# Weight sums and their stores held in program order, ten steps apart, begun one group of weights later, in a streaming encoder step

## The chip, the core and the metric

The kernel runs on one core of one Trainium2 chip. The metric is the device time of one execution in microseconds (us), as the median of several executions. Engines are called by their names or by the profile's short ones: TensorE (PE, with PEld for its weight loads), VectorE (DVE), ScalarE (ACT), GpSimd (POOL), SyncE (SP). A letter q behind a name means the engine's sequencer, which issues DMAs.

## What is computed

One inference step of one encoder layer, in float32, for two groups of requests that share the weights: a prompt of 2048 rows and 8 samples of 16 rows, 17 tiles of 128 rows of width 1024 in all.

```python
h = rms_norm(x, norm_g[0])
z = h @ w_in                       # 1024 x 3592, split among the heads
att = band_attention(...)          # 8 heads of 64, own chunk of 64 and 8 before it
hb = mlstm(...)                    # 4 heads of 128, a matrix memory along the sequence
x = x + rms_norm(concat(att, mlstm_out) @ w_out, norm_g[1])
u = rms_norm(x, norm_g[2]) @ w_up  # 1024 x 5632
y = b_conv + causal_conv3(u)
x = x + rms_norm((gelu(y_gate) * y_up) @ w_down, norm_g[3])
```

Caches and states are outputs too. The change touches none of the arithmetic.

## The kernel before, in words

Every float32 product is made as three products of high and low parts in a rounded format (`mm3`, lines 95 to 97): of each weight that is loaded, ScalarE makes the high part and VectorE the low one.

The two products of the FFN use seven block products in place of eight (a scheme after Strassen), and so need sums and differences of quarters of `w_up` and `w_down`. These do not depend on the data, but they are inputs' sums and have to be made in the kernel: `weight_sums` makes them once, while the first part of the layer runs, and writes them to DRAM (`wsd` and `wtd`), from where the FFN loads them later. Each of the 22 blocks of `w_up` and 11 of `w_down` is one unit. A unit has four loads of a quarter (128 x 512, line 1189, on SyncE's queue, into buffers `wsum0` to `wsum3` with two copies each), four combines (`tensor_tensor` on VectorE, line 1193, each in place, the later ones using the results of the earlier) and four stores (line 1197, on SyncE's queue). A table `acts` says in which step of a generator each of these is called: four loads in four steps, the combines eleven steps behind the loads, the stores three steps behind the combines, and the next unit eleven steps behind this one.

The first part of the layer is a loop over 28 groups of weights (14 groups of columns of `w_in`, for each half of the rows; `seq`). A group's product yields after every half of an accumulation: 18 or 16 times for a group of row tiles (`va`, `vo`), 12 times for a transposed one (`qk`, `qb`). At each yield the loop calls one step of the next group's load (line 1163, with its split at 1169 and 1170), one step of the weight sums, sometimes one of a row tile's norm (`norm_tile`, load at 214, Square on ScalarE at 218, scaling on VectorE at 221, then eight transposes on TensorE), and then `pump`, which lets steps of two other streams go: attention (loads of a head's `qraw`, `kraw` and `vraw` at 336, 339 and 353, split at 344 to 358, scores and softmax at 384 to 421) and the matrix memory (lines 640 to 790). A step of the sums counts as no work there, so the order in which everything else is called does not depend on the sums.

What is called is not yet the order on the engines. A scheduler takes all instructions, and by a timing model of its own puts each on its engine's queue when it holds it to be ready, mostly in the order of calls. Each engine then works through its queue in order. `tc.keep_in_program_order(ins)` adds one edge: `ins` does not come ahead of the one instruction that was called before it on the same engine. It adds no wait, and that other instruction itself may still be moved ahead of its own predecessors. The loads of the sums already have this edge.

At the end of the loop come the output projection (`wo`) with the norms, and then the FFN in three blocks of rows (`ua`, `ub`, `uec` are the accumulators of its first product, `dnm` and `dn` of its second).

Of the kernel before, what the change touches and what calls it, by code (L numbers as in the profile page):

```python
# [44 lines left out]
def hymba_step(ctx: ExitStack, tc: tile.TileContext, I: dict, O: dict):  # L45
    nc = tc.nc
# [213 lines left out]
    def group_rows(wh, wl, half, chunks, dst, name, width=256, out=None):  # L260
        for ci, tiles in enumerate(HALVES[half]):
            for j, t in enumerate(tiles):
                ch = chunks[ci]
                acc = ps_mm(f"{name}_{t}")
                for k in range(KT):
                    w = slice(k * width, (k + 1) * width)
                    tt = slice(j * P, (j + 1) * P)
                    mm3(acc[:, :width], ch[:, 0, k, tt], ch[:, 1, k, tt], wh[:, w], wl[:, w],
                        start=(k == 0), stop=(k == KT - 1))
                    if k % 4 == 3:  # L270
                        yield 1.3, 0.0
                stage = pa.tile([P, 384], F32, tag="st", name=f"{name}_st{t}", bufs=2)
                evac_scaled(stage[:, :256], acc[:, :256], None)
                if width > 256:
                    nc.vector.tensor_copy(gates[:, gate_ix(t), :], acc[:, 256:width])
                s = 4 if t == SAMPLE else t // 4
                nc.scalar.dma_start(dst[s][:, 0 if s == 4 else t % 4, :], stage[:, :256])
                if out is not None and s >= 3:
                    nc.scalar.dma_start(out[s - 3][:, 0 if s == 4 else t % 4, :], stage[:, :256])
# [536 lines left out]
    def prep(units):  # L816
        yield units
        yield FLUSH
# [230 lines left out]
    def quad(name):  # L1049
        return ffn.p3.tile([P, 512], F32, tag="q", name=name, bufs=11)  # L1050
# [101 lines left out]
    def load_group(gi):  # L1152

        i = SRC[GROUPS[gi]]
        src, n = (I["w_in0"], 2112) if i == 0 else (I["w_in1"][i - 1], 2048)
        h = wpool.tile([P, 2112], F32R, tag="wh", name=f"wi{i}_h{gi}", bufs=2)
        l = wpool.tile([P, 2112], F32R, tag="wl", name=f"wi{i}_l{gi}", bufs=2)

        def steps():
            q = n // 2  # L1160
            for s in range(2):
                raw = pr.tile([P, 1056], F32, tag="wraw", name=f"wi{i}_raw{s}")
                nc.sync.dma_start(raw[:, :q], src[:, s * q:(s + 1) * q])
                yield 0.0, 0.0
                yield 0.0, 0.0
                for e in range(2):
                    c = slice(s * q + e * q // 2, s * q + (e + 1) * q // 2)
                    r = raw[:, e * q // 2:(e + 1) * q // 2]
                    nc.scalar.copy(h[:, c], r)
                    nc.vector.tensor_tensor(l[:, c], r, h[:, c], op=ALU.subtract)  # L1170
                    yield 0.0, 0.6

        return h, l, steps()

    def weight_sums():


        add, sub = ALU.add, ALU.subtract
        up = ((2, 3, 2, add), (3, 0, 3, sub), (0, 2, 0, sub), (1, 1, 0, sub))
        down = ((0, 1, 0, sub), (1, 2, 1, sub), (2, 2, 0, sub), (3, 3, 2, sub))  # L1180
        todo = [(I["w_up"][f], wsd[f], up, f"u{f}") for f in range(NF)]
        todo += [(I["w_down"][i], wtd[i], down, f"d{i}") for i in range(NF // 2)]
        acts = defaultdict(list)
        for n, (src, dst, plan, nm) in enumerate(todo):
            t = []

            def load(i, src=src, t=t, nm=nm):
                t.append(pr.tile([P, 512], F32, tag=f"wsum{i}", name=f"wsum{nm}_{i}", bufs=2))
                tc.keep_in_program_order(nc.sync.dma_start(t[i], src[:, i * 512:(i + 1) * 512]))

            def combine(e, plan=plan, t=t):
                o, x, y, op = plan[e]
                nc.vector.tensor_tensor(t[o], t[x], t[y], op=op)

            def store(e, dst=dst, plan=plan, t=t):
                o = plan[e][0]
                nc.sync.dma_start(dst[:, o * 512:(o + 1) * 512], t[o])

            for i in range(4):
                acts[11 * n + i].append(lambda i=i, f=load: f(i))  # L1200
                acts[11 * n + 11 + i].append(lambda i=i, f=combine: f(i))
                acts[11 * n + 14 + i].append(lambda i=i, f=store: f(i))
        for step in range(max(acts) + 1):
            for act in acts[step]:
                act()
            yield 0.0, 0.0

    def norm_steps(half):

        for ci, tiles in enumerate(HALVES[half]):  # L1210
            ch = phT.tile([P, 2, KT, 384], F32R, tag="hT", name=f"hT{half}_{ci}", bufs=3)
            chunks.append(ch)
            for j, t in enumerate(tiles):
                norm_tile(t, ch, j, ps_big)
                yield 0.9, 2.5
# [10 lines left out]
    next(norms)  # L1226
    load_bias()
    sums = weight_sums()
    for n_, (half, gi) in enumerate(seq):
        wh, wl, _ = pend  # L1230
        split = iter([])
        if n_ + 1 < len(seq):
            pend = load_group(seq[n_ + 1][1])
            split = pend[2]
        g = GROUPS[gi]
        i = int(g[2])
        nm = f"{g}_{half}"
        if g[:2] == "va":
            it = group_rows(wh, wl, half, chunks, vd[i], nm, 264 if gi == 0 else 256,
                            [O["v_prompt"][i], O["v_sample"][i].unsqueeze(1)])  # L1240
        elif g[:2] == "qk":
            it = group_T(wh, wl, half, chunks, [qTd[i], kTd[i]], [-(DA ** -0.5), None], nm,
                         [None, [O["k_prompt"][i], O["k_sample"][i]]])
        elif g[:2] == "qb":
            it = group_T(wh, wl, half, chunks, [[t_[:, c, :] for t_ in qkbd[i]] for c in range(2)],
                         [None, DH ** -0.5], nm)
        else:
            it = group_rows(wh, wl, half, chunks, vobd[i], nm)
        if half == 0 and gi == 13:
            chunks = []  # L1250
            norms = norm_steps(1)
        if n_ == len(seq) - 1:
            out = project([0, 1, 2, 3, 4, 5, 6, 7, SAMPLE, 8, 9, 10, 11, 12, 13, 14, 15])
            split = w_out_steps()
            next(split)
            next(out)
        for u, (pe, dve) in enumerate(it):
            ahead = []
            if n_ < len(seq) - 1 or u >= 6:
                ahead.append(next(split, (0.0, 0.0)))  # L1260
            if n_ == len(seq) - 1 and u == 12:
                ahead.append(next(out))
            if n_:
                ahead.append(next(sums, (0.0, 0.0)))
            if (half == 0 and gi == 13 and u >= 6 and u % 2 == 0) or (gi == 0 and u % 2 == 0):
                ahead.append(next(norms, (0.0, 0.0)))
            pump(pe + sum(a[0] for a in ahead), dve + sum(a[1] for a in ahead))
        for _ in split:
            pass
        if n_ == len(seq) - 1:  # L1270
            for _ in sums:
                pass
        if gi == 0:
            if half == 0:
                nc.sync.dma_start(bgate, I["b_gate"].broadcast_to([P, 8]))
                nc.sync.dma_start(gatt, I["g_att"])
                heads.append(build_bias)
                mems.append(lambda: prep(prep_sample()))
            mems.append(lambda half=half: prep(prep_prompt(half)))
        if g[:2] == "qk":  # L1280
            attention(i, half)
            if half == 0 and i == 3:
                heads.insert(len(heads) % 4, lambda: attention_sample(0, EARLY))
            if half == 1 and i == 0:
                heads.insert(len(heads) % 4, lambda: attention_sample(EARLY, DB))
        if g[:2] == "vo":
            mems.append(lambda i=i, half=half: mlstm(i, half))
            if half == 0:
                mems.append(lambda i=i: mlstm_sample(i))
# [145 lines left out]
    for b, tiles in enumerate(FBLOCKS):  # L1435
        last = b == len(FBLOCKS) - 1
        nt = len(tiles)
        n = HALF[b]
# [180 lines left out]
        if not last:  # L1619
# [4 lines left out]
            for q in range(42):  # L1624
# [25 lines left out]
                for j in range(3):  # L1650
# [4 lines left out]
                    elif p == D2:  # L1655
                        o = quad(f"c11_{b}_{j}")
# [7 lines left out]
                    elif p == D4:  # L1664
                        o = quad(f"c21_{b}_{j}")
# [160 lines left out]
```

## Time and profile before

| | us |
|---|---|
| median of 3 runs | 2860.12 |
| lowest, highest | 2860.08, 2869.72 |
| the profiled execution | 2870.22 |
| its span in the trace | 2868.5 |
| mean granted clock of TensorE in it | 0.982 |

The profile comes from one execution, whose own time is 2870.22 us; its span, from the first instruction to the last, is 2868.5 us. In a table of stretches each engine has its busy time in us with the number of instructions in brackets, then PEclk, the mean clock that TensorE was granted as a share of full speed, the busy share of the DMA engines, and GB/s. A row of waits reads: engine, what it wants to write and at which line, then who was waited for; the total in us, how often, and the longest. A row of the timeline reads: start, length, engine, line, operation, output and inputs, count, and in square brackets how long the engine had been idle before, and what released it.

### The profile page before, as it was taken

The page shows a single profiled execution, that of the slowest core. Times are in us where ns is not written, and L with a number is a line of the kernel's source. Part 1 is how long each engine was busy: PE and PEld are TensorE (multiplying, and loading weights), DVE is VectorE, ACT ScalarE, POOL GpSimd, SP SyncE. Part 2 cuts the span into 40 slices and gives each one's busy share as a digit, 9 for nine tenths or more (in the row PEclk, how much of TensorE's full clock was granted, in tenths as well). Part 3 has the DMA queues.
Part 4 walks back from the last instruction along what each step waited for, and adds up shares of the span by engine and source line. Part 5 has one row for each costly group of instructions (what it writes and reads, how often), then busy time and mean ns, then how long its engine had stood idle before and what let it go on. Part 6 is the DMA issues. An engine that isn't in the chain of part 4 may idle for free.

```text
span 2868.5 us, 47580 instructions
## 1 busy us (share of the span) xinstructions
PE 2726.6 (95%) x16389; PEld 2540.8 (89%) x16389; DVE 1977.6 (69%) x3640; ACT 1439.0 (50%) x2908; POOL 436.3 (15%) x876
## 2 busy tenths in 40 slices
PE   7899999989889999898999999999999999999998
PEld 7799999888889997776899998889999878999877
DVE  5355555656656567676588888858888885888765
ACT  4254544534435556553355555754545565555543
POOL 1000000111100001223411110011111121222221
PEclk9999999999999999998999999999999999999999
DMA  5755567568877576435565556774555797555586
GB/s 172 221 170 175 173 194 219 184 213 266 270 255 218 166 212 210 141 100 165 190 211 179 165 181 200 265 226 155 175 177 166 244 324 245 171 177 180 170 297 204
DMA packets 371346, 575.50 MB, mean 201 GB/s; under 512 B 60611, under 2 KB 176799, under 8 KB 370975
## 3 DMA queue, kind: packets, MB, share of 16 engines
q1 hardware_dynamic: 332510, 538.62, 59.6%
q10 hardware_dynamic: 38592, 33.83, 3.5%
q8 instruction: 129, 2.11, 0.3%
q14 instruction: 115, 0.93, 0.1%
HBM read 424.24 MB, written 151.21 MB: 201 GB/s over the span
## 4 chain that ended last, share of the span: by engine, by line
PE 49%; DVE 3%; DMA 3%; issue 2%; ACT 1%; POOL 1%; SPq 0%; DVEq 0%; ACTq 0%; POOLq 0%
PE uec L95 6%; PE uec L96 6%; PE uec L97 6%; PE ua L97 3%; PE ua L96 3%; PE ua L95 3%; PE dn L95 3%; PE dn L97 3%; PE dn L96 3%; PE dnm L97 2%; PE dnm L95 2%; PE dnm L96 2%; PE ub L96 1%; PE ub L97 1%; PE ub L95 1%
## 5 line engine op out<-in xcount | busy, mean ns | idle before, releaser
L95 PE MATMUL uec<-B,wuh 128*128 128x384 f32 (+1 forms) x720 | 234.3, 327 | 1.5 <-DVE uu L1451 1.5
L96 PE MATMUL uec<-B,wuh 128*128 128x384 f32 (+1 forms) x720 | 235.2, 327 | 0.0
L97 PE MATMUL uec<-B,wul 128*128 128x384 f32 (+1 forms) x720 | 234.2, 327 | 0.0
L1298 ACT CAST wuh<-wu 128x512 fp32r<-128x512 f32 x315 | 172.9, 617 | 81.0 <-PE uec L96 79.2
L1299 DVE TENSOR_TENSOR wul<-wu,wuh 128x512 fp32r<-128x512 f32 x315 | 202.9, 685 | 2.9 <-DMA x2d<-mx 2.9
L95 PE MATMUL dn<-wdh,gh 128*128 128x512 f32 x422 | 168.1, 398 | 12.0 <-ACT gh L1298 9.0
L96 PE MATMUL dn<-wdl,gh 128*128 128x512 f32 x422 | 168.1, 398 | 0.0
L97 PE MATMUL dn<-wdh,gl 128*128 128x512 f32 x422 | 163.9, 402 | 0.2 <-DVE gl L1299 0.2
L95 PE MATMUL vo<-wi_h,hT 128*128 128x256 f32 x544 | 157.3, 289 | 3.4 <-ACT vo_st L226 3.3
L96 PE MATMUL vo<-wi_l,hT 128*128 128x256 f32 x544 | 156.4, 287 | 0.0
L97 PE MATMUL vo<-wi_h,hT 128*128 128x256 f32 x544 | 155.2, 285 | 0.0
L1299 DVE TENSOR_TENSOR wdl<-wdr,wdh 128x512 fp32r<-128x512 f32 x198 | 128.4, 697 | 30.7 <-ACT wdh L1298 30.6
L95 PE MATMUL qk<-hT,wi_h 128*128 128x384 f32 (+1 forms) x384 | 130.8, 341 | 11.2 <-ACT qk_st L226 8.3
L408 DVE TENSOR_TENSOR ptl<-pt,pth 128x640 fp32r<-128x640 f32 (+4 forms) x128 | 93.4, 736 | 68.3 <-ACT pth L407 67.6
L396 ACT ACTIVATE tmp<-tmp,mn 128x640 f32<-128x640 f32 (+4 forms) x128 | 97.6, 763 | 84.8 <-DVE mn L395 78.4
L1298 ACT CAST wdh<-wdr 128x512 fp32r<-128x512 f32 x198 | 111.9, 618 | 54.1 <-DMA wdr<-in_w_down 22.5
L95 PEld LDWEIGHTS uec<-B,wuh 128*128 128x128 f32 x720 | 135.0, 188 | 2.7 <-DVE uu L1451 2.5
L96 PEld LDWEIGHTS uec<-B,wuh 128*128 128x128 f32 x720 | 135.2, 188 | 0.1
L97 PEld LDWEIGHTS uec<-B,wul 128*128 128x128 f32 x720 | 135.1, 188 | 0.0
L96 PE MATMUL qk<-hT,wi_h 128*128 128x384 f32 (+1 forms) x384 | 130.3, 339 | 0.0
L97 PE MATMUL qk<-hT,wi_l 128*128 128x384 f32 (+1 forms) x384 | 130.1, 339 | 0.0
L95 PE MATMUL qb<-hT,wi_h 128*128 128x384 f32 (+1 forms) x384 | 127.8, 333 | 1.9 <-ACT qb_st L228 1.1
(428 smaller groups left out, 8904.9 us busy)
## 6 DMA issues: line engine op xcount, KB each, us to landing
wu<-wsd SPq DMA_DIRECT2D x264, 256.0 KB, 3.8
wu<-in_w_up SPq DMA_DIRECT2D x198, 256.0 KB, 4.0
wdr<-in_w_down SPq DMA_DIRECT2D x110, 256.0 KB, 6.1
wi_raw<-in_w_in SPq DMA_DIRECT2D x52, 512.0 KB, 5.8
gq<-gsd SPq DMA_DIRECT2D x62, 384.0 KB, 5.2
wsumu<-in_w_up SPq DMA_DIRECT2D x88, 256.0 KB, 5.2
wsd<-wsumu SPq DMA_DIRECT2D x88, 256.0 KB, 4.4
wdr<-wtd SPq DMA_DIRECT2D x88, 256.0 KB, 6.0
```

The source lines that it names most:

```text
L95: nc.tensor.matmul(out, ah, bh, start=start, stop=False, skip_group_check=onto)
L96: nc.tensor.matmul(out, ah, bl, start=False, stop=False, skip_group_check=onto)
L97: nc.tensor.matmul(out, al, bh, start=False, stop=stop, skip_group_check=onto)
L396: nc.scalar.activation(tmp[:, :n], tmp[:, :n], AF.Exp, bias=mn, scale=-1.0, accum_out=rsum[:, i % 4, hh:hh + 1])
L408: nc.vector.tensor_tensor(s.ptl[:, sl, qc], ptv, s.pth[:, sl, qc], op=ALU.subtract)
L1298: nc.scalar.copy(h, r)
L1299: nc.vector.tensor_tensor(l, r, h, op=ALU.subtract)
```

## The change

Four things change in the sums, and nothing else in the code:

- the combine and the store get `keep_in_program_order`, as the loads have it;
- units are called 10 steps apart instead of 11 (the combines stay 11 steps behind the loads of their unit);
- the stores are called two steps behind their combines instead of three;
- the sums begin with the third group of weights instead of the second (`n_ > 1`), 30 yields after the start instead of 18. 32 intervals of 10 and the last store's 16 steps make 337 steps, from yield 30 to 367; before it was 32 × 11 + 17 + 1 = 370 steps, from 18 to 388, of 396.

```diff
             def combine(e, plan=plan, t=t):
                 o, x, y, op = plan[e]
-                nc.vector.tensor_tensor(t[o], t[x], t[y], op=op)
+                tc.keep_in_program_order(nc.vector.tensor_tensor(t[o], t[x], t[y], op=op))
 
             def store(e, dst=dst, plan=plan, t=t):
                 o = plan[e][0]
-                nc.sync.dma_start(dst[:, o * 512:(o + 1) * 512], t[o])
+                tc.keep_in_program_order(nc.sync.dma_start(dst[:, o * 512:(o + 1) * 512], t[o]))
 
             for i in range(4):
-                acts[11 * n + i].append(lambda i=i, f=load: f(i))
-                acts[11 * n + 11 + i].append(lambda i=i, f=combine: f(i))
-                acts[11 * n + 14 + i].append(lambda i=i, f=store: f(i))
+                acts[10 * n + i].append(lambda i=i, f=load: f(i))
+                acts[10 * n + 11 + i].append(lambda i=i, f=combine: f(i))
+                acts[10 * n + 13 + i].append(lambda i=i, f=store: f(i))
...
-            if n_:
+            if n_ > 1:
                 ahead.append(next(sums, (0.0, 0.0)))
```

The scheduler moves other instructions with these, since its model of the time changes. Three places show it. The first is SyncE's queue near the start, in the first group of weights, before: `xr_710` is the load of the sample's rows, `wi_raw` are halves of the next groups' weights, `wsumu_0` to `wsumu_2` the quarters of the first unit (a number at the end of a name only counts the tiles made).

```order
L1163 DMA wi_raw_822<-in_w_in 128x1024
L1189 DMA wsumu_0_824<-in_w_up 128x512
L1189 DMA wsumu_1_838<-in_w_up 128x512
L1189 DMA wsumu_2_899<-in_w_up 128x512
L214 DMA xr_710<-in_x_sample 128x1024
L1163 DMA wi_raw_963<-in_w_in 128x1024
```

And the same place of SyncE's queue after:

```order
L1163 DMA wi_raw_822<-in_w_in 128x1024
L214 DMA xr_710<-in_x_sample 128x1024
L1163 DMA wi_raw_955<-in_w_in 128x1024
L304 DMA relrow<-ext 128x767 x4
L327 DMA nb_0_1246<-relrow 128x640
L327 DMA nb_0_1317<-relrow 128x640
L1163 DMA wi_raw_1159<-in_w_in 128x1024
L1189 DMA wsumu_0_1161<-in_w_up 128x512
```

The first unit's loads, which stood ahead of the sample's rows, now stand five loads of other things behind them. On ScalarE's queue the Square of those rows (line 218) has at the same time moved ahead by one tile: it now stands in front of the copy of the accumulator `va_0_5` (line 226), where it stood in front of that of `va_0_6`.

The second place is VectorE's queue in the first of the matrix memory's heads (`num`, `ad` and `cst` belong to it), near 425 us in the profile of before; `wi_l` is a low part of weights. Before:

```order
L706 TENSOR_TENSOR num_4_4598<-num_4_4598,ma_4_1_4635 128x129
L640 SCALAR_TENSOR_TENSOR ad_4_4672<-num_4_4598 128x2
L1193 TENSOR_TENSOR wsumu_2_4802<-wsumu_3_4835,wsumu_2_4802 128x512
L641 TENSOR_TENSOR ad_4_4672<-ad_4_4672,colsp 128x2
L1170 TENSOR_TENSOR wi_l_5910<-wi_raw_5924,wi_h_5909 128x512
```

The same place of VectorE's queue after:

```order
L703 SCALAR_TENSOR_TENSOR cst_319<-cst_319,dec_1119,ma_4_1_4635 128x129
L694 TENSOR_TENSOR w_6_1_4667<-ms_6_1_4664,w_6_1_4667 128x128
L494 TENSOR_SCALAR hgms_4909<-hgms_4909 128x128
L884 RECIPROCAL srs_4291<-srs_4291 128x1
L706 TENSOR_TENSOR num_4_4597<-num_4_4597,ma_4_1_4635 128x129
L640 SCALAR_TENSOR_TENSOR ad_4_4672<-num_4_4597 128x2
L641 TENSOR_TENSOR ad_4_4672<-ad_4_4672,colsp 128x2
```

The combine between the two steps of `ad` is gone from there; combines of other units stand elsewhere in the queue.

The third place is SyncE's queue where a unit's stores (`wsd`) stand among the loads of attention heads (`qraw`, `kraw`, `vraw`), in the third pair of weights' columns. Before:

```order
L1197 DMA wsd_241<-wsumu_3_1929 128x512
L336 DMA qraw_0_2102<-qTd_0_99 64x512 x2
L339 DMA kraw_0_0_2103<-kTd_0_82 64x512 x2
L1197 DMA wsd_241<-wsumu_0_1804 128x512
L1197 DMA wsd_241<-wsumu_1_1840 128x512
```

After, in that region:

```order
L1197 DMA wsd_240<-wsumu_2_1826 128x512
L1189 DMA wsumu_3_2282<-in_w_up 128x512
L353 DMA vraw_1_1_2349<-vd_1_115 128x4x64
L1197 DMA wsd_240<-wsumu_0_1743 128x512
L336 DMA qraw_1_2465<-qTd_1_100 64x512 x2
L339 DMA kraw_1_0_2466<-kTd_0_82 64x512 x2
```

A store stands ahead of a head's loads in both; in the new order the stores of a unit are spread more among them.

## The prediction

> **What bounds the kernel now.** I read the page's busy line first, then the table of stretches, then who waits for whom on VectorE and SyncE, and last the timeline around TensorE's gaps.
>
> ```profile
> PE 2726.6 (95%) x16389; PEld 2540.8 (89%) x16389; DVE 1977.6 (69%) x3640; ACT 1439.0 (50%) x2908; POOL 436.3 (15%) x876
> core 0: us, PE busy (x) PEld busy (x) DVE busy (x) ACT busy (x) POOL busy (x), PEclk, DMA share, GB/s
> 0.00:40.00 40.00, 29.09 (x217) 27.99 (x218) 26.83 (x41) 24.09 (x39) 9.21 (x31) 1.00 0.70 221
> 40.00:130.00 90.00, 72.99 (x397) 68.88 (x397) 30.57 (x98) 18.62 (x42) 1.32 (x6) 0.89 0.62 180
> 130.00:1330.00 1200.00, 1117.51 (x7643) 1052.49 (x7643) 720.36 (x1633) 597.95 (x1455) 144.60 (x335) 0.98 0.64 197
> 1330.00:2868.50 1538.50, 1507.00 (x8137) 1391.46 (x8135) 1199.84 (x1869) 798.32 (x1374) 281.19 (x505) 0.99 0.63 204
> ```
>
> TensorE sets the time, so the change is worth what it takes out of TensorE's gaps and out of the stretches with a low granted clock. The sums live in the first 1110 us (rows below); behind 1330 us the order of instructions changes in a few dozen rows only. From 40 to 1330 us TensorE is idle for (90 − 73.0) + (1200 − 1117.5) = 99.5 us. That is the whole stock from which a gain can come, beside the clock.
>
> ```profile
> DVE wsumu L1193 <- DMA wsumu<-in_w_up: 60.0, 26, 7.7
> DVE wsumd L1193 <- DMA wsumd<-in_w_down: 13.4, 8, 3.4
> SPq L1197 <- DVE wsumu L1193: 36.4, 23, 4.8
> SPq L1189 <- DMA wsd<-wsumu: 15.2, 11, 2.8
> L1193 DVE TENSOR_TENSOR wsumu<-wsumu,wsumu x88: 669/691/694, 91.6 to 815.8; 128x512 f32<-128x512 f32 x88
> L1193 DVE TENSOR_TENSOR wsumd<-wsumd,wsumd x44: 670/691/851, 816.6 to 1104.3; 128x512 f32<-128x512 f32 x44
> ```
>
> VectorE stands still 60.0 + 13.4 = 73.4 us in front of a combine whose load has not landed: the scheduler had put the combine right behind its load. A combine itself takes 0.691 us, and the number of combines stays 132, so no work goes; only the standing can go.
>
> **The change, part by part.** *Combines tied to program order.* The combine now stands where the code calls it, eleven steps behind its load, unless the one instruction that it is tied to has itself been moved up. That hole matters: in the listing of the order with semaphores, 80 of 132 combines name a DMA's semaphore before and 48 after. So at least 1 − 48/80 = 40% of the waits go, and at most all, since some of the 48 find their load landed long ago. I take 70%. What a wait costs TensorE is read at the places where a gap follows it:
>
> ```profile
> 427.17 0.69 DVE L1193 TENSOR_TENSOR wsumu<-wsumu,wsumu 128x512 f32<-128x512 f32 x1 [1.90 <-DMA wsumu<-in_w_up]
> 430.44 0.35 PE L700 MATMUL ma<-cst,mqk 128*128 128x129 f32 x1 [1.54 <-DVE cst L703]
> 432.04 0.44 PE L67 MATMUL spt<-ident,stmp 128*128 128x128 f32 x2 [0.91 <-ACT stmp L882]
> 583.84 0.69 DVE L1193 TENSOR_TENSOR wsumu<-wsumu,wsumu 128x512 f32<-128x512 f32 x1 [1.69 <-DMA wsumu<-in_w_up]
> 586.13 0.39 PE L97 MATMUL va<-wi_h,hT 128*128 128x264 f32 x1 [2.10 <-DVE hT L201]
> 815.78 0.69 DVE L1193 TENSOR_TENSOR wsumu<-wsumu,wsumu 128x512 f32<-128x512 f32 x1 [7.75 <-DMA wsumu<-in_w_up]
> 816.59 3.01 DVE L1193 TENSOR_TENSOR wsumd<-wsumd,wsumd 128x512 f32<-128x512 f32 x4
> 820.26 0.79 PE L96 MATMUL sot<-svl,sph 128*128 128x512 f32 x1 [2.50 <-DVE svl L904]
> 828.30 0.49 PE L95 MATMUL sot<-svh,sph 16*128 16x512 f32 x1 [1.22 <-ACT svh L903]
> ```
>
> The gaps add up to 1.54 + 0.91 + 2.10 + 2.50 + 1.22 = 8.3 us; the other waits, most of the 73.4 us, are followed by no gap, because TensorE had matmuls of the dense projection to go on with. Behind three of these places the granted clock falls to about a half:
>
> ```profile
> 46.90:57.10 10.20, 6.67 (x23) 6.27 (x24) 2.75 (x4) 1.79 (x5) 0.74 (x2) 0.51 0.08 27
> 432.60:436.00 3.40, 3.40 (x19) 3.40 (x18) 2.28 (x9) 2.34 (x10) 1.63 (x6) 0.54 0.95 265
> 586.20:589.60 3.40, 3.40 (x17) 3.40 (x18) 2.10 (x8) 0.77 (x3) 0.00 (x0) 0.54 0.55 104
> 818.30:825.10 6.80, 4.84 (x17) 4.36 (x18) 3.62 (x6) 0.00 (x0) 1.20 (x3) 0.52 0.89 287
> 122.00:125.40 3.40, 3.40 (x14) 3.40 (x13) 0.00 (x0) 0.48 (x1) 0.00 (x0) 0.54 0.99 349
> ```
>
> The loss is the length times one minus the clock: 3.40 × 0.46 = 1.6 us twice and 6.80 × 0.48 = 3.3 us, together 6.5. So this part holds 8.3 + 6.5 = 14.8 us, and 70% of it is 10.3 us (bounds 5.9 and 14.8).
>
> The Trainium skill, "TensorE: Matmul & The Clock Gate", section "What's actually happening", says the clock is halved after at least one idle window of about 3.4 us. By that rule gaps of 0.9 to 2.5 us would cost no clock and this part would be worth 70% of the gaps alone. The rows at 432.60 and 586.20 speak against it: 2.45 us of gaps and a single one of 2.10 us are each followed by 3.4 us at 0.54.
>
> *Begun one group later.* Before, three loads of the first unit stand on SyncE's queue right ahead of the sample's rows:
>
> ```profile
> 34.63 1.37 SPq L1189 DMA_DIRECT2D wsumu<-in_w_up  x3
> 36.27 0.67 SPq L214 DMA_DIRECT2D xr<-in_x_sample  x1
> 39.18 0.37 ACT L226 COPY va_st<-va 128x256 f32<-128x256 f32 x1 [1.88 <-PE va L97]
> 45.90 1.06 ACT L218 ACTIVATE hT<-xr 128x1024 fp32r<-128x1024 f32 x1 [6.35 <-DMA xr<-in_x_sample]
> 49.33 0.47 PE L67 MATMUL hT_pt<-ident,xr 128*128 128x128 f32 x1 [4.39 <-DVE xr L221]
> wu<-wsd SPq DMA_DIRECT2D x264, 256.0 KB, 3.8
> wsumu<-in_w_up SPq DMA_DIRECT2D x88, 256.0 KB, 5.2
> ```
>
> Now they stand behind it. Three times 256 KB at the 221 GB/s of that stretch is 3.6 us by which the rows land sooner: the Square starts at 45.90 − 3.6 = 42.3. But the scheduler now puts that Square ahead of the copy that was made at 39.18, so the copy slips to 42.3 + 1.06 = 43.4 and ends at 43.7. TensorE, which began its last row tile when it finished the one before (half of the way from the copy's 39.2 to 49.33 − 4.39 = 44.9, about 42.0), now begins it at 43.7, 1.7 us later, and ends at 46.7. The transposes follow at once: 49.33 − 46.7 = 2.6 us gained. Of the 10.20 × 0.49 = 5.0 us lost behind that gap at half clock I take half, 2.5. Sum 5.1 us; the bounds are 0 (the copy's new wait eats it) and 4.39 + 5.0 = 9.4.
>
> *Fewer of its transfers around 120 us.* Here ScalarE waits for an attention head's loads, with sums' loads in flight beside them:
>
> ```profile
> 117.60 2.14 DVE L1193 TENSOR_TENSOR wsumu<-wsumu,wsumu 128x512 f32<-128x512 f32 x3 [4.70 <-DMA wsumu<-in_w_up]
> 120.23 0.62 ACT L348 CAST kh<-kraw 128x512 fp32r<-128x512 f32 x1 [7.66 <-DMA vraw<-vd]
> 121.59 0.45 PE L95 MATMUL qk<-hT,wi_h 128*128 128x384 f32 x1 [4.28 <-ACT qk_st L226]
> ```
>
> This gap with its 3.40 × 0.46 = 1.6 us of clock is 5.9 us. The sums' traffic is delayed there by one group but not gone, and VectorE's wait is beside the chain, not in it; I take a third, 2 us (bounds −2, for the same loads falling on the next head, and 5.9).
>
> *Ten steps instead of eleven, stores two steps behind their combine.* The same 132 loads, combines and stores in 330 instead of 363 steps: VectorE's share for them rises by a tenth for as long as they run, from 132 × 0.691 = 91 us in the 1013 us between 91.6 and 1104.3, 9.0%, to 9.9%. VectorE is busy 720 of 1200 us there, so I cost it at nothing; if that cover is gone it is 0.9% of those 1013 us, 9 us at most. The sums end some 20 steps sooner, which only frees VectorE.
>
> *Stores tied to program order.* SyncE works its queue in order, and behind a store that waits for its combine stand the loads of the next head and of the next weights. Before, such waits sum to 36.4 us in 23, the longest 4.8 us, and none of TensorE's gaps above hangs on one. Now the combine isn't held up by its load, but the store can't be moved away from what follows. I take nothing; bounds are a gain of 2 us and the loss of the second rival below.
>
> Sum: 10.3 + 5.1 + 2 = 17.4 us. The profiled execution took 2870.2 us, which is 10 above the median of 2860.1 and equal to the highest of the three runs; the saving is set against the median: 2860.1 − 17.4 = 2842.7, forecast **2843 us**.
>
> **The rivals.** *1. Nothing comes of it.* VectorE waits where it has nothing urgent behind the combine, and the stalls of TensorE that I count are replaced by stalls a few instructions on. For it: of 73.4 us of waits only 8.3 us show as gaps. Against: the clock rows behind them. With two thirds of my sum given back, 2860.1 − 5.8 = 2854. The Trainium skill, "Perfetto Trace Analysis", section "Identifying Performance Opportunities", bids one improve the most-contended engine; by that rule a wait on VectorE (69% beside 95%) would be worth nothing. The trace agrees for most of the waits and not for the five gaps.
>
> *2. SyncE's queue takes the wait over (slower).* The tied store stands between the loads of one head and of the next, and stalls SyncE until VectorE gets to the combine. Decisive is whether the loads behind have slack: the gap at 121.59, where they had none, cost 5.9 us. Three such places in the 33 units use up the forecast's 17.4 us; six give 2860.1 − 17.4 + 6 × 5.9 = 2878. Against: none of the 23 waits of before had that effect.
>
> *3. It doesn't do what it says.* The tie is to one predecessor only, and 48 combines still name a DMA. With 40% of the waits gone and the start's term alone beside it: 0.4 × 14.8 + 5.1 = 11.0, 2849.
>
> *4. No clock to win.* If gaps below 3.4 us cost no clock, as the clock rule above has it, and the low clocks come back wherever they fall, the gaps alone remain: 0.7 × 8.3 + 2.6 + 1.4 (a third of 4.28) = 9.8, 2850.
>
> **How the numbers follow.** The forecast 0.56; rival 1 0.17, rival 2 0.13, rival 3 0.08, rival 4 0.06. A measurement of this kernel can tell about 0.5%, 14.3 us, from no change. The forecast alone counts as faster (0.56), rivals 1, 3 and 4 as the same (0.31), rival 2 as slower (0.13). The low end takes all of the three parts, 9.4 + 14.8 + 5.9 = 30.1 us, and the 10 us between the runs: 2820. The high end holds rivals 1, 3 and 4 and some of rival 2, at 8 us above the median: 2868.
>
> **What would show it.** The FFN's first product marks the end of the stretch in which anything moves:
>
> ```profile
> L95 PE MATMUL ua<-B,wuh x360: 303/336/341, 1425.6 to 2689.8; 128*128 128x384 f32 x120, 128*128 128x320 f32 x60
> ```
>
> Right: VectorE's wait for the sums' loads at 10 to 35 us instead of 73.4; no gap of 4 us at 45 us in front of the sample's transposes; fewer stretches at half clock before 1330 us, and this product starting at about 1425.6 − 17.4 = 1408 us. Wrong: SyncE's waits at line 1197 well over 36.4 us with ScalarE waiting for an attention head's loads behind them; TensorE's idle time from 40 to 1330 us near 99 us with other names; or a difference behind the FFN's start, where I expect none.

## The result, and the profile after

The changed kernel took 2846.74 us in the median of 5 runs (2839.61 to 2848.92), the kernel before, run beside it, 2866.2 us (2860.08 to 2874.68, 5 runs). The ratio is 0.992 with a 95% interval of 0.990 to 0.994: 0.8% faster; the medians differ by 19.5 us. The forecast was 2843 us, 17.4 us under the median that before had had in its first three runs. The profiled execution of the changed kernel took 2848.63 us, its span is 2846.9.

The page's busy line and the table of stretches of the changed kernel, with the same columns as before:

```profile
PE 2716.3 (95%) x16389; PEld 2535.1 (89%) x16389; DVE 1974.8 (69%) x3640; ACT 1437.2 (50%) x2908; POOL 442.4 (16%) x876
40.00:130.00 90.00, 80.29 (x473) 76.98 (x472) 29.80 (x101) 26.03 (x60) 3.05 (x9) 0.92 0.58 169
130.00:1330.00 1200.00, 1118.34 (x7659) 1053.82 (x7660) 730.93 (x1643) 594.86 (x1452) 153.48 (x341) 0.98 0.65 199
```

The row from 40 to 130 us is the first surprise: in it TensorE did 473 matmuls where it had done 397. Who waits for the sums now, on VectorE and on SyncE:

```profile
DVE wsumu L1193 <- DMA wsumu<-in_w_up: 10.1, 5, 4.2
DVE wsumd L1193 <- DMA wsumd<-in_w_down: 1.2, 2, 0.8
SPq L1197 <- DVE wsumu L1193: 31.4, 22, 6.2
SPq L1197 <- DVE wsumd L1193: 8.4, 10, 2.4
SPq L1189 <- DMA wsd<-wsumu: 18.7, 13, 4.7
SPq L1189 <- DMA wtd<-wsumd: 10.6, 8, 3.8
```

VectorE's 73.4 us have become 11.3, at the lower end of what I had expected to see. So if those waits had been what TensorE lost, the gain would lie between 140 and 1050 us. Where it does lie is read at three points: the first product of the `qb` groups, the FFN's first (`ua`), and between them a mark, the point from which TensorE has 1900 matmuls left to the FFN's first. Before, the mark is passed at 1050.2 us:

```profile
L95 PE MATMUL qb<-hT,wi_h x384: 277/336/529, 235.8 to 1043.2; 128*128 128x384 f32 x160, 128*128 128x256 f32 x32
235.80:1050.20 814.40, 771.34 (x5485) 742.06 (x5485) 472.79 (x1124) 390.99 (x948) 74.01 (x221) 0.99 0.69 213
1050.20:1425.60 375.40, 339.04 (x1903) 287.57 (x1902) 252.90 (x454) 187.40 (x453) 108.32 (x156) 0.95 0.50 161
```

And after, where it is passed at 1046.1 us (a row counts every matmul that runs at all in its stretch, hence 1902 or 1903):

```profile
L95 PE MATMUL qb<-hT,wi_h x384: 277/337/530, 223.3 to 1052.0; 128*128 128x384 f32 x160, 128*128 128x256 f32 x32
L95 PE MATMUL ua<-B,wuh x360: 303/336/341, 1407.5 to 2667.4; 128*128 128x384 f32 x120, 128*128 128x320 f32 x60
223.30:1046.10 822.80, 769.36 (x5484) 741.59 (x5484) 490.38 (x1168) 398.56 (x973) 81.36 (x225) 0.99 0.72 220
1046.10:1407.50 361.40, 333.83 (x1902) 283.35 (x1901) 237.85 (x416) 177.37 (x430) 105.01 (x152) 0.97 0.48 156
```

At the first `qb` the changed kernel is 235.8 − 223.3 = 12.5 us ahead. At the mark it is 4.1 ahead: 8.4 us have been lost again, on the stretch in which I had forecast a gain of 10.3. TensorE's idle time there has grown from 814.4 − 771.3 = 43.1 us to 822.8 − 769.4 = 53.4. From the mark to the FFN the kernel wins 375.4 − 361.4 = 14.0 us, so that the FFN begins 18.1 us sooner. The other 3.5 us of the spans' difference lie behind the FFN's start; they are less than the 9 us by which executions of one kernel differ here, and I make nothing of them.

### The profile page after: what moved, and what is told of

It reads as the page before. It is cut to its first block, busy times and chain, and to the rows that moved or that the text cites. A ratio compares the mean times of both kernels' runs of the same rounds, so it can differ in the third digit from the quotient of the medians.

```text
span 2846.9 us, 47564 instructions
## 1 busy us (share of the span) xinstructions
PE 2716.3 (95%) x16389; PEld 2535.1 (89%) x16389; DVE 1974.8 (69%) x3640; ACT 1437.2 (50%) x2908; POOL 442.4 (16%) x876
## 4 chain that ended last, share of the span: by engine, by line
PE 49%; DVE 3%; DMA 3%; issue 2%; POOL 1%; ACT 1%; SPq 0%; DVEq 0%; POOLq 0%; ACTq 0%
PE uec L95 6%; PE uec L96 6%; PE uec L97 6%; PE ua L97 3%; PE ua L96 3%; PE ua L95 3%; PE dn L97 3%; PE dn L95 3%; PE dn L96 3%; PE dnm L97 2%; PE dnm L96 2%; PE dnm L95 2%; PE ub L96 1%; PE ub L97 1%; PE ub L95 1%
## 5 line engine op out<-in xcount | busy, mean ns | idle before, releaser
L1298 ACT CAST wdh<-wdr 128x512 fp32r<-128x512 f32 x198 | 112.3, 618 | 49.9 <-DMA wdr<-in_w_down 17.4
L395 DVE CUSTOM_DVE_ANT_0 tmp<-s,nb 128x640 f32<-128x640 f32 (+4 forms) x128 | 94.0, 736 | 55.0 <-PE s L385 54.3
```

The lines of the kernel that those rows point to most:

```text
L395: nc.vector.tensor_tensor_reduce(o_, s_, b_, 1.0, 3e38, ALU.add, ALU.min, accum_out=mn)
L1298: nc.scalar.copy(h, r)
```

## The experiments

Two theories were put against each other. **Theory A** is the prediction's: the ties take VectorE's waits away and with them TensorE's gaps, and the later begin frees the sample's rows. **Theory B**, the rival: the saving comes from the later begin and from another order at the end, and the ties by themselves bring nothing. After the first four kernels a **theory C** was added: the start is a mechanism; what lies behind it is another order from the scheduler in each variant, whose worth doesn't follow from VectorE's waits.

All kernels differ from the kernel before only in the lines shown or, where an edit has been shown already, named. A measured ratio is that to the kernel before, run beside it, with its 95% interval; waits and starts come from one profiled execution of each kernel.

**Ties only.** The two ties of the change, with spacing and begin as before.

```diff
-                nc.vector.tensor_tensor(t[o], t[x], t[y], op=op)
+                tc.keep_in_program_order(nc.vector.tensor_tensor(t[o], t[x], t[y], op=op))
...
-                nc.sync.dma_start(dst[:, o * 512:(o + 1) * 512], t[o])
+                tc.keep_in_program_order(nc.sync.dma_start(dst[:, o * 512:(o + 1) * 512], t[o]))
```

> Combines and stores tied, spacing 11 steps, sums begin with the second group as before. Theory A (the ties take VectorE's waits away and with them TensorE's gaps): VectorE's waits for the sums' loads fall from 73.4 us to under 25 us, and the time falls by about 10 us, a ratio near 0.9964, all of it between 140 and 1050 us. Theory B (the saving comes from the later begin and from the order of attention at the end, the ties alone bring nothing): the waits fall as well, but the ratio is between 0.999 and 1.003.

Measured: 0.9935 (0.9914 to 0.9956), waits 23.0 us. A larger gain than either theory expected; but 235.8 − 228.1 = 7.7 of the 12.9 us by which the FFN starts sooner were won before the first `qb`, where A sees nothing. From `qb` to the mark, where A has its gain, this kernel needs 814.0 us, as before (814.4):

```profile
228.10:1042.10 814.00, 774.32 (x5485) 748.33 (x5484) 475.75 (x1132) 392.67 (x954) 80.75 (x221) 0.97 0.69 214
```

**Later begin only.**

```diff
-            if n_:
+            if n_ > 1:
```

> The sums begin with the third group, nothing else is changed. Theory A: the sample's rows land about 3.6 us sooner, the gap of 4.39 us at 45 us is gone, 5 to 7 us saved, ratio near 0.998; VectorE's waits stay near 73 us. Theory B: the first 140 us are worth 12.5 us as in the changed kernel, ratio near 0.9956, and what the changed kernel has beyond that needs the order at the end.

Measured: 0.9866 (0.985 to 0.9882), 2827.28 us, the fastest of the kernels that compute everything, and faster than the changed kernel, whose interval ends at 0.990. Its VectorE waits are those of before:

```profile
DVE wsumu L1193 <- DMA wsumu<-in_w_up: 57.8, 22, 10.7
DVE wsumd L1193 <- DMA wsumd<-in_w_down: 14.2, 8, 4.6
L95 PE MATMUL ua<-B,wuh x360: 303/336/341, 1385.9 to 2649.5; 128*128 128x384 f32 x120, 128*128 128x320 f32 x60
```

72.0 us of waits and an FFN that begins 39.7 us sooner: this gain, the largest of the kernels that make the sums, came without touching VectorE's waits for the sums. Neither theory had this size.

**Spacing only** (10 steps, stores 13 steps behind the loads instead of 14).

```diff
-                acts[11 * n + i].append(lambda i=i, f=load: f(i))
-                acts[11 * n + 11 + i].append(lambda i=i, f=combine: f(i))
-                acts[11 * n + 14 + i].append(lambda i=i, f=store: f(i))
+                acts[10 * n + i].append(lambda i=i, f=load: f(i))
+                acts[10 * n + 11 + i].append(lambda i=i, f=combine: f(i))
+                acts[10 * n + 13 + i].append(lambda i=i, f=store: f(i))
```

> Units 10 steps apart, stores two steps behind the combines, no ties, begun with the second group. Theory A: nothing, ratio 0.998 to 1.002, VectorE's waits near 73 us. Theory B: the sums end 33 steps sooner, VectorE is free of them before the end of the projection, so the part from 1050 to 1400 us gets shorter by up to 15 us, ratio near 0.996.

Measured: 1.0034 (1.0021 to 1.0046), slower by a third of a per cent, which neither theory had. The FFN begins at 1425.4, as before, but two things cancel in that:

```profile
235.30:1060.40 825.10, 775.55 (x5486) 746.47 (x5485) 480.42 (x1135) 390.72 (x951) 73.49 (x221) 0.98 0.70 216
1060.40:1425.40 365.00, 331.77 (x1903) 281.51 (x1902) 247.41 (x443) 187.49 (x452) 106.44 (x156) 0.98 0.49 151
```

Up to the mark 825.1 − 814.4 = 10.7 us are lost, and behind it 375.4 − 365.0 = 10.4 are won. So B's shorter end is there, and its ratio isn't.

**The change without its ties** (later begin and spacing, as in the two diffs above).

> The changed kernel without the two ties. Theory A: the 10 us of the ties are missing, ratio near 0.9965 instead of 0.992, VectorE's waits near 73 us. Theory B: the ties bring nothing, ratio 0.991 to 0.994 as with them.

Measured: 0.9964 (0.9947 to 0.998), as A expected, and outside B's range. Set against the changed kernel (0.9902 to 0.9939), the ties here go with 0.4%, near the size that A gives them. But they do not go with it where A has it: from `qb` to the mark the changed kernel needs 3.7 us more than this one. And the later begin alone is a whole per cent better than this.

**Ties and later begin, spacing 11.**

> Both ties and the begin with the third group, units 11 steps apart as before. The later begin alone gave 0.987 and the ties alone 0.9935. Theory A (parts that add up): 0.980. Theory C (beyond the start, each variant gets another order from the scheduler, whose worth does not follow from the waits): anywhere from 0.982 to 0.997, not the product.

Measured: 0.9942 (0.9926 to 0.9958). The two parts that each gain alone gain together no more than the ties alone (0.9935) and less than the later begin alone; they don't add up, and A's 0.980 is far off.

**Begun one yield later**, a control.

```diff
+        for _ in range(1):
+            yield 0.0, 0.0
         for step in range(max(acts) + 1):
```

> The sums begin one yield later (about 3 us), spacing and all else as before; a control for what a meaningless shift does. Theory A: no change beyond 0.1%, ratio 0.999 to 1.001. Theory C: the whole order from 100 to 1300 us is laid anew, and the ratio may lie anywhere from 0.988 to 1.005.

Measured: 0.9928 (0.9906 to 0.9949). A shift of one yield is worth as much as the change under study. It isn't quite the meaningless shift that was meant: two of the first unit's loads instead of three now stand ahead of the sample's rows, and `qk` starts at 48.4 instead of 53.0.

**Begun six yields later** (`range(6)` in the same place).

> The sums begin six yields later, half of the change's delay. Theory A: the sample's rows are free of the sums' loads already, so 5 to 13 us are saved in the first 140 us and nothing after, ratio 0.9955 to 0.998. Theory C: the same saving in the first 140 us, and another 10 us up or down after them.

Measured: 0.9904 (0.9888 to 0.9919), a larger gain than A allowed; 18.7 of the 28.1 us by which the FFN begins sooner are won before the first `qb`.

**First unit four steps later**, the other 32 where they were.

```diff
-                acts[11 * n + i].append(lambda i=i, f=load: f(i))
+                acts[(11 * n or 4) + i].append(lambda i=i, f=load: f(i))
```

(and the same in the two lines below it).

> Only the first unit is called four steps later, so that its loads stand behind the sample's rows; the other 32 units are called where they were. Theory A: the gap of 4.4 us before the sample's transposes goes with its half clock, 5 to 9 us saved by 60 us, and this stays to the end, ratio near 0.9975. Theory C: the same by 60 us, then the order after is another one as well, by up to 10 us either way.

Measured: 0.9952 (0.9931 to 0.9972). One unit in 33 moved, and with it the larger part of the saving: more than A's 0.9975, and with the FFN 17.7 us sooner.

**Later begin without combines.**

```diff
-                nc.vector.tensor_tensor(t[o], t[x], t[y], op=op)
+                pass
```

> Begun with the third group, and the 132 combines are left out: the quarters are loaded and stored again as they are, so the outputs of the FFN are not the reference's, and 91 us of VectorE's work and all its 73 us of waits for the sums are gone, while SyncE's transfers stay. Theory A (VectorE's waits hold TensorE up): well below the later begin alone (0.9866), 0.976 to 0.981. Theory C: somewhere from 0.982 to 0.996, no better than kernels that have all combines and their waits.

Measured: 0.9848 (0.9816 to 0.988). With all of VectorE's work and waits for the sums gone, it cannot be told from the later begin alone (0.985 to 0.9882), and A's 0.976 to 0.981 isn't reached. It doesn't rule out the 10.3 us of the prediction's sum, which would be 0.9866 − 0.0036 = 0.983. The profiled execution, 10 us under this kernel's median, starts the FFN 9.2 us sooner than the later begin's, and 7.7 us of that are won between `qb` and the mark (796.5 against 804.2). So VectorE's whole part in the sums may cost something of that size. The kernel isn't a clean one either: its stores now wait on SyncE for their loads to land, 143.2 us in all.

**Later begin, combines tied, stores not.**

> Begun with the third group, only the combines tied. The later begin alone gave 0.9866, with both ties 0.9942. If the tied stores on SyncE's queue are what lost the difference, this kernel stays at 0.984 to 0.988. If the tied combines lose it, 0.993 to 0.995. Theory C: neither has a price of its own, 0.984 to 0.996, with VectorE's waits under 30 us in any case.

Measured: 0.991 (0.9876 to 0.9944). The interval overlaps both answers: which of the ties takes back the later begin's gain stays open.

**Begun 24 yields later, and three** (`range(24)`, `range(3)`).

> The sums begin 24 yields later than before (1, 6 and 12 later gave 0.9928, 0.9904 and 0.9866); the last 16 steps are called in a row at the end. If the delay itself pays, step by step: 0.980 to 0.984. If only the sample's rows and the first heads' loads gain by it: by 140 us some 13 to 19 us are saved, and the rest is open, 0.984 to 0.995.

> The sums begin three yields later. If the delay itself pays, step by step, this lies between the kernels with 1 and 6 yields, 0.990 to 0.993. Theory C: 6 to 8 us are saved by 60 us and the rest is open, 0.984 to 0.998.

Measured: 0.9944 (0.9924 to 0.9964) and 0.9943 (0.9921 to 0.9966). With 1, 3, 6, 12 and 24 yields the ratios are 0.9928, 0.9943, 0.9904, 0.9866 and 0.9944: the delay doesn't pay by its length.

All of them side by side; starts are those of the first matmul of `qk` (the second group), `qb` and `ua` in the profiled execution, waits are sums of the rows at lines 1193 (for the sums' loads) and at 1197 and 1189 (for combines, and for a store to land), all but the ratio in us:

| kernel | ratio | VectorE waits | SyncE waits | qk starts | qb starts | ua starts | qb to ua |
|---|---|---|---|---|---|---|---|
| before | 1 | 73.4 | 62.4 | 53.0 | 235.8 | 1425.6 | 1189.8 |
| spacing only | 1.0034 | 83.5 | 69.3 | 51.8 | 235.3 | 1425.4 | 1190.1 |
| ties only | 0.9935 | 23.0 | 48.4 | 51.5 | 228.1 | 1412.7 | 1184.6 |
| first unit 4 later | 0.9952 | 68.7 | 60.9 | 47.5 | 224.6 | 1407.9 | 1183.3 |
| begun 1 later | 0.9928 | 65.0 | 45.6 | 48.4 | 226.6 | 1409.4 | 1182.8 |
| begun 3 later | 0.9943 | 54.5 | 49.2 | 48.4 | 224.6 | 1412.6 | 1188.0 |
| begun 6 later | 0.9904 | 60.7 | 54.5 | 48.6 | 217.1 | 1397.5 | 1180.4 |
| later begin (12) | 0.9866 | 72.0 | 43.5 | 48.0 | 220.5 | 1385.9 | 1165.4 |
| begun 24 later | 0.9944 | 61.3 | 61.4 | 48.8 | 220.8 | 1409.3 | 1188.5 |
| late, combines tied | 0.991 | 23.8 | 73.1 | 49.0 | 222.0 | 1410.8 | 1188.8 |
| late, both tied | 0.9942 | 21.1 | 70.9 | 47.5 | 221.0 | 1410.8 | 1189.8 |
| late, spacing 10 | 0.9964 | 68.8 | 61.8 | 48.4 | 222.9 | 1410.6 | 1187.7 |
| the change | 0.9921 | 11.3 | 69.1 | 48.6 | 223.3 | 1407.5 | 1184.2 |
| late, no combines | 0.9848 | 0 | 4.9 | 48.1 | 222.6 | 1376.7 | 1154.1 |

Three things stand out. Every kernel that begins later, by one yield or by 24 or with its first unit alone, starts `qk` at 47.5 to 49.0 us; the three that begin as before, at 51.5 to 53.0. From `qb` to `ua` the kernels with 11 to 24 us of VectorE's waits need 1184 to 1190 us, those with 54 to 84 need 1165 to 1190: among kernels that make the sums, no gain with fewer waits. And the 18.1 us by which the changed kernel's FFN begins sooner are hardly more than the 13 to 18 that seven of the ten other kernels with a later begin have, tied or not, 9 to 15 of them by the first `qb`.

What each edit does on the two sides of the mark is read from kernels that differ in that edit alone (us by which the stretch gets longer; less is a gain):

| edit added | from | to | `qb` to mark | mark to `ua` |
|---|---|---|---|---|
| both ties | before | ties only | −0.4 | −4.8 |
| both ties | later begin | late, both tied | +10.4 | +14.0 |
| both ties | late, spacing 10 | the change | +3.7 | −7.2 |
| spacing 10 | before | spacing only | +10.7 | −10.4 |
| spacing 10 | later begin | late, spacing 10 | +14.9 | +7.4 |
| spacing 10 | late, both tied | the change | +8.2 | −13.8 |

These are single executions, and the order is laid anew in each kernel: the five that only begin 1 to 24 yields later need 804.2 to 821.0 us from `qb` to the mark, where before needs 814.4. So a figure counts only where its sign holds in all three rows.

## Why the prediction was right

**The later begin: the mechanism right.** The start of the changed kernel, on SyncE, ScalarE and TensorE:

```profile
36.88 0.33 SPq L214 DMA_DIRECT2D xr<-in_x_sample  x1
41.49 1.06 ACT L218 ACTIVATE hT<-xr 128x1024 fp32r<-128x1024 f32 x1 [3.59 <-DMA xr<-in_x_sample]
42.55 0.35 ACT L226 COPY va_st<-va 128x256 f32<-128x256 f32 x1
43.15 0.39 PE L95 MATMUL va<-wi_h,hT 128*128 128x264 f32 x1 [0.51 <-DVE gates L275]
46.16 1.03 PE L67 MATMUL hT_pt<-ident,xr 128*128 128x128 f32 x8
46.90:57.10 10.20, 8.44 (x56) 7.99 (x55) 2.19 (x9) 2.45 (x5) 0.00 (x0) 1.00 0.06 19
```

The Square starts at 41.49 (forecast 42.3), the copy behind it does slip and does put a gap ahead of the last row tile, of 0.51 us instead of the forecast 1.7, and the transposes follow without a gap at 46.16 (46.7) instead of 49.33. In the 10.2 us that had run at a clock of 0.51, TensorE is granted 1.00 and does 56 matmuls instead of 23. What the whole is worth shows behind that stretch, where both kernels run at full clock again, in the 20th matmul of `qk`, first before and then after:

```profile
58.35 0.34 PE L96 MATMUL qk<-hT,wi_h 128*128 128x384 f32 x1
51.94 0.33 PE L96 MATMUL qk<-hT,wi_h 128*128 128x384 f32 x1
```

That is 6.4 us, for a term forecast at 5.1 within bounds of 0 and 9.4. All eleven kernels that begin later are 6.0 to 7.5 us ahead at this matmul. The two others that begin as before are 1.7 and 2.2 ahead of the one execution of before, so 4 to 6 us is what the later begin can be said to be worth. 3.2 of the 6.4 are the transposes' earlier start. The clock gave the other 3.2 or so, not half of 5.0: the product 10.20 × 0.49 also counts time in which TensorE stood idle, and it was busy for 6.67 of the 10.20 us, 6.67 × 0.49 = 3.3. The same slip is in the stretch at 818.30 us, where TensorE was busy for 4.84 of 6.80 us: 2.3 us instead of 3.3.

One reading of mine was loose. The sample's rows are not issued sooner: at 36.27 before, at 36.88 after. It is from the issue to the Square that the time went, 9.6 us before and 4.6 after. So the three loads ahead of them cost their transfers, not their places in the queue.

From there to the first `qb` another 6.1 us are won, where the sum had 2 (bounds −2 and 5.9). That this comes from the later begin isn't shown: the kernel with the ties only, which begins as before, wins 6.0 us on the same stretch. The start is the one term that the experiments confirm one by one.

The clock rule of the Trainium skill's "TensorE: Matmul & The Clock Gate" ("What's actually happening") asks for an idle window of about 3.4 us. The trace agrees at neither of two places. In the gap of 4.39 us, which began at 44.94, the clock fell after little more than 2 us (the mean of 0.56 in the first row below puts the fall at 47.2); and at 586 us half clock follows a single gap of 2.10 us. Nor does the length of a gap decide it: one of 2.54 us that ended at 560.97 was followed by full clock. The rows of before, the second for that last gap:

```profile
46.90:49.33 2.43, 0.00 (x0) 0.00 (x1) 1.51 (x3) 0.78 (x4) 0.74 (x2) 0.56 0.30 105
560.97:571.20 10.23, 9.85 (x82) 9.64 (x82) 7.32 (x16) 7.18 (x19) 1.48 (x4) 1.00 0.84 299
```

**The ties: the step that failed.** "So this part holds 8.3 + 6.5 = 14.8 us, and 70% of it is 10.3 us" assumed that a gap behind a wait goes when the wait goes, and that nothing takes its place. The waits went, by 85%. The gain of 10.3 us shows in none of the three pairs of kernels that differ in the ties: with the ties added, the way from `qb` to the mark gets longer by −0.4, +10.4 and +3.7 us. Other gaps came. In the changed kernel two of them, 11.5 us together, are larger than all five old ones (8.3):

```profile
SPq L1189 <- DMA wsd<-wsumu: 4.7, 1, 4.7
641.63 0.82 SPq L1189 DMA_DIRECT2D wsumu<-in_w_up  x2
642.88 0.33 SPq L493 DMA_DIRECT2D hgms<-in_g_mlstm  x1
646.78 0.23 DVE L494 TENSOR_SCALAR hgms<-hgms 128x128 f32<-128x128 f32 x1 [5.74 <-DMA hgms<-in_g_mlstm]
648.74 0.80 PE L700 MATMUL ma<-cst,mqk 128*128 128x129 f32 x2 [5.37 <-DVE num L706]
646.90:653.70 6.80, 4.96 (x23) 4.88 (x24) 4.43 (x19) 3.29 (x12) 0.88 (x2) 0.50 0.18 62
```

The first row is the wait on SyncE from 636 to 642 us: a load of the sums has to wait until the store from the same buffer has landed. Behind it on the queue stands a small load of the matrix memory's scales; VectorE waits 5.74 us for that one, and TensorE 5.37 us for VectorE, with 6.8 us at a clock of 0.50 after it. The second place:

```profile
834.92 4.48 SPq L1197 DMA_DIRECT2D wtd<-wsumd  x5
839.77 1.68 SPq L336 DMA_DIRECT2D qraw<-qTd  x2
851.55 0.62 ACT L344 CAST qs<-qraw 128x512 fp32r<-128x512 f32 x1 [7.84 <-DMA wtd<-wsumd]
853.04 0.87 PE L384 MATMUL s<-kh,qs 128*128 128x320 f32 x2 [6.16 <-ACT vo_st L226]
851.70:858.50 6.80, 5.46 (x24) 5.33 (x25) 2.08 (x3) 1.88 (x4) 0.00 (x0) 0.50 1.02 288
```

Five stores take SyncE 4.48 us, and behind them the head's `qraw` is issued at 839.77 and used at 851.55, 11.8 us later, where 4.2 us is the median from such an issue to its landing in this run. Both places are kin to the second rival, SyncE's queue and transfers taking the wait over, but not by its mechanism: at neither does a store stand waiting for its combine for more than 0.5 us. With (4.96 + 5.46) × 0.50 = 5.2 us of clock they come to some 16.7 us. They are not shown to come from the ties: three kernels without ties have a gap of that size on this stretch too (5.00 us at 794.69 with the later begin alone, 4.42 at 804.88 with one yield, 5.07 at 810.50 with three).

**Ten steps: put at nothing, and not nothing.** From `qb` to the mark the kernels with ten steps need 8.2 to 14.9 us more in all three pairs, with ties or without; spacing alone loses 10.7. I had named 9 us as the most that it could cost, if VectorE's cover were gone. So the 8.4 us that the changed kernel lost there go with the spacing more than with the ties. By what path is open: VectorE's busy time on that stretch rises from 472.8 to 490.4 us, and no run took that apart from the order.

**What paid instead.** The 14.0 us between the mark and the FFN stood in no term of the sum. The busy time of TensorE falls from 339.0 to 333.8 us for as many matmuls (the clock, 0.95 to 0.97) and its idle time from 36.4 to 27.6. Two of the gaps that are gone stood ahead of transposes for the output projection:

```profile
1152.95 1.01 PE L67 MATMUL mT_pt<-ident,mr 128*128 128x128 f32 x4 [3.02 <-DVE mr L987]
1200.95 1.11 PE L67 MATMUL mT_pt<-ident,mr 128*128 128x128 f32 x4 [2.42 <-DVE mr L987]
```

The last combine starts at 1059.2 us instead of 1104.3, so the sums' earlier end, which I had counted as freeing only VectorE, may be the cause. Two of the three pairs for the spacing have a gain of this size there (10.4 and 13.8 us), the third a loss of 7.4; and the later begin alone, with eleven steps, needs 361.2 us there, as little as the changed kernel. So the cause stays open.

So the sum was near by luck: from `qb` to the mark 10.3 us were forecast and 8.4 lost, and this was made up by a first stretch of 12.5 us instead of 7.1 and by 14.0 us for which nothing was forecast. Of the rivals, the first, that nothing comes of the ties, is the one that the pairs bear out. The Trainium skill's "Perfetto Trace Analysis" ("Identifying Performance Opportunities") bids one look at the most contended engine. The trace agrees here more than I allowed, as with the ties alone 50 us of VectorE's waits went and TensorE's stretch from `qb` to the mark stayed as it was (814.0 us against 814.4). The third did not happen (the waits fell to 15%). Of the fourth, one half fails, since gaps under 3.4 us did cost clock; the other half, that the low clocks come back wherever they fall, holds from `qb` to the mark: by the trace's clock records 20.5 us at half clock before, 23.9 after.

**Forecast points on the profile.** VectorE's waits 10 to 35 us: 11.3. No gap of 4 us before the sample's transposes: none. Fewer stretches at half clock before 1330 us: nine instead of twelve. FFN's first product at 1408: 1407.5. SyncE's waits at line 1197, named as a sign of being wrong if well over 36.4 us: 31.4. TensorE's idle time from 40 to 1330 us, named as another if near 99 us with other names: (90 − 80.29) + (1200 − 1118.34) = 91.4 us, and with other names for the most part. That sign told the truth about the ties.

## What to carry to other kernels

A wait on an engine that is not the bound costs only what reaches the bound, so take it away in an experiment before it is put into the sum; here 62 us of waits went and their stretch grew slower. Read such a stretch between the same two points of the bound engine's work, in kernels that differ in one edit: only so did the loss show itself as the spacing's and not the ties'. A load that nobody needs yet, issued just ahead of one that is needed now, can cost its transfer and clock on top; here three such loads cost 4 to 6 us, a term that could be read from four rows and that held in all eleven kernels that start the sums later. In pricing a stretch at half clock, count only the part of it in which the engine is busy. Where a scheduler lays the order, run a control that shifts something small: here one yield was worth 0.7%, as much as the whole change, of which only the start could be traced; a change of that size is no evidence for the reason that it was made for.

## What the runs showed that I had not expected

The same later begin that gives 0.9866 alone gives 0.9942 with both ties and 0.9964 with the spacing. From `qb` to the FFN the kernels that make the sums spread from 1165 to 1190 us. What sets this isn't known. The fastest of them has the fewest of SyncE's waits at lines 1189 and 1197 (43.5 us), and those with 69 to 73 us need 1184 to 1190; but those with 45.6 to 49.2 need 1183 to 1188, and the kernel without combines, whose SyncE waits 143.2 us at line 1197 for loads, needs 1154.1, the least of all. The version to keep is the later begin alone.
